# A two-layer hybrid decoder step: sums of weight pieces, normalized x and quarter sums move from GpSimd to VectorE, and the first group of eight hidden tiles is computed without Strassen

## The chip, the cores and the metric

The kernel runs on one core of a Trainium2 chip. The engines are TensorE (PE: matmuls; PEld is its weight load), VectorE (DVE), ScalarE (ACT), GpSimd (POOL) and SyncE (SP, which issues the weight loads). Each works off a queue of its own in order and waits on semaphores. The metric is device time in microseconds (us) of one execution; less is better.

## The reference, cut to what matters

Two groups of tokens, 512 of a prompt and 8 x 8 of samples, go through two layers. A layer is a mixer (untouched here) and then a gated MLP with a convolution over three tokens on the gate:

```
h = rmsnorm(x, norm_ffn[l])
gate, fbuf = causal_dwconv(h @ w_ffn_gate[l], ffn_conv_w[l], st_fconv[l])
x = x + (jax.nn.silu(gate) * (h @ w_ffn_up[l])) @ w_ffn_down[l]
```

with `rmsnorm(x, g) = x * rsqrt(mean(x * x) + EPS) * g`, D_MODEL = 1024 and D_FF = 2816. All is float32.

## The kernel before

**Layout.** Features lie on the 128 partitions, the 576 tokens in the free dimension; x is 8 tiles of 128 features (`KT`), the hidden layer 22 tiles (`FT`). Tokens are halved into two products of 288 columns (`HALVES`). A float32 product is made of three matmuls in fp32r: each operand is split into a high part (`whi`, `xh`, `fh`, `nh`, `hh`), a rounding copy on ScalarE, and a low part (`wlo`, `xl`, `fl`, `nl`, `hl`), a subtraction on VectorE, and hi x hi, hi x lo and lo x hi are added up in PSUM (`mm3`).

**Weights.** `plan` lists all weight pieces in the order in which TensorE uses them. A piece is one output tile by half of its input features, [128, 4, 128], and feeds 24 matmuls (4 blocks, 2 token halves, 3 parts). `_Weights` loads pieces by SyncE into rings (`wraw`, `wrax`), splits each into whi and wlo (`_split`; 6 buffers of each) and runs ahead of TensorE (`pump`).

**The MLP.** The hidden tiles go in three groups (`FGS`: 8, 8 and 6). For each group there are gate and up products (tile m = 2j is the gate of hidden tile j, m = 2j + 1 its up), then the down products of this group, which add onto x. Gate tail of j: convolution in three steps (`gcv`, the first on ScalarE), tanh on ScalarE, the product that makes silu (`gth`). Up tail of j: product of gate and up from PSUM (`gp`, one for each token half), then the split into `hh` and `hl`, which the down products read. The down products begin with two output tiles on hidden tiles 0 to 3 of the group, then the same two on 4 to 7 (mode `kouter`).

**Raw, then normalized.** The norm needs all of x, so the first `RAW` = 3 hidden tiles of a layer (six output tiles) are computed from x without its factor R (`fh`, `fl`), and R is applied afterwards (`scaled`, and two products in the gate tail). Meanwhile the normalized x is made: a scaled copy on ScalarE into the space of hh and hl, a product with R on GpSimd, then the split into `nh` and `nl` (`normed`).

**Strassen on the gates.** From hidden tile `PLAIN` = 6 on, gates are made two at a time by Strassen's scheme on quarters (`quad`): 7 products of 12 matmuls instead of 8. Its weight operands are sums of pieces (`post` in `plan`, computed by `_Weights._next` on GpSimd, 4 per pair: `wsum` and three times `wraw`), its x operands are sums of quarters of the normalized x (`quarters`: four differences on GpSimd, then a split into the space of `fh` and `fl`). In the reading of the products one addition into `gpad` is on GpSimd too.

**What sets the order.** The code is run once to record the instructions. A planner holds modelled clocks of the engines; streams (generators such as `gate_tail`, `up_tail`, `quarters`) are advanced between matmuls (`tick`), the one with the earliest modelled start first, and streams that share the 5 temporary tiles (`take`, `give`) wait for a free one. The recorded order of each engine is then fixed, and each engine works off its own in order. `drain` advances streams until the named ones are done: of the quarter sums before the first Strassen pair, of all up tails of a group before the down products read hidden tiles 4 to 7.

Of the kernel before, what the change touches and what calls it, by code (L numbers as in the profile page):

```python
# [27 lines left out]
RAW, PLAIN = 3, 6  # L28
# [72 lines left out]
class _Weights:  # L101
# [53 lines left out]
    def _next(self):  # L155
# [9 lines left out]
        for dst, a, b, op in p["post"]:  # L165
# [3 lines left out]
            self.nc.gpsimd.tensor_tensor(out=self.raw[dst], in0=self.raw[a], in1=self.raw[b], op=op)  # L169
# [14 lines left out]
    def pump(self):  # L184

        while self.ns < len(self.pieces) and self.ns <= self.at + self.BUFS - 2 \
                and self.upto[self.ns] - self.upto[max(self.at, 0)] <= 4:
            src = self.pieces[self.ns]["src"]
            if self.there.get(src, 0.0) > self.nc.vector.plan.now:
                break  # L190
            self._next()
# [49 lines left out]
class _Trunk:  # L241
# [1353 lines left out]
    def build(self):  # L1595
# [94 lines left out]
        for l in range(L):  # L1690
# [55 lines left out]
            for gi, g in enumerate(groups):  # L1746
# [9 lines left out]
            early, late = ([self.px.tile([128, 4, NT], dt, name=n + i, tag=n + i) for n in ("hh", "hl")]  # L1756
                           for i, dt in (("0", F32R), ("1", F32)))
            hid = list(map(_Halves, early))
# [5 lines left out]
            def whole(k):  # L1764

                return late[k // 4][:, k % 4]

            def normed(k):
                w = whole(k)
                S.activation(out=w, in_=xr[:, k], func=AF.Copy, scale=self.p(l, "gffn", k, k + 1))  # L1770
                yield
                nc.gpsimd.tensor_tensor(out=w, in0=w, in1=self.R, op=ALU.mult)
                yield
                S.activation(out=nh[:, k], in_=w, func=AF.Copy)
                yield
                V.tensor_tensor(out=nl[:, k], in0=w, in1=nh[:, k].bitcast(F32), op=ALU.subtract)

            def quarters(k):

                u, w = whole(k), whole(k + 4)  # L1780
                (b11, b12), (b21, b22) = (u[:, 0:HC], u[:, HC:NT]), (w[:, 0:HC], w[:, HC:NT])
                P = nc.gpsimd
                P.tensor_tensor(out=b11, in0=b12, in1=b11, op=ALU.subtract)
                P.tensor_tensor(out=b12, in0=b22, in1=b12, op=ALU.subtract)
                P.tensor_tensor(out=b22, in0=b22, in1=b11, op=ALU.subtract)
                P.tensor_tensor(out=b21, in0=b21, in1=b22, op=ALU.subtract)
                yield
                for i, y in enumerate((u, w)):
                    y = y.rearrange("p (h i) -> p h i", h=2)
# [3 lines left out]
                    V.tensor_tensor(out=tl, in0=y, in1=th.bitcast(F32), op=ALU.subtract)  # L1793

# [335 lines left out]
```

## Time and profile before

| | |
|---|---|
| median of 3 runs | 1524.88 us (1524.59 to 1526.04) |
| profiled execution | 1523.45 us, of it 1521.7 us from the first to the last instruction (the span) |
| PE busy in the span | 1478.8 us (97%), 11428 matmuls |
| DVE busy | 1063.8 us (70%) |
| ACT busy | 680.3 us (45%) |
| POOL busy | 346.5 us (23%) |
| TensorE's mean granted clock | 0.988 of 2.4 GHz |

Matmuls overlap in TensorE, so one of 288 columns has about 0.29 us in the profile while the next starts 0.13 us later; dense work is read from starts, or from the chain of work, not from the busy share. The rows further down are of the first layer; the second layer's MLP lies 747.5 us later.

### The profile page before, as it was taken

Reading aid. Unit: us, or ns where it says so; the run is one execution under the profiler, and the core shown is the slowest. Engines: PE = TensorE matmul, PEld = TensorE weight load, DVE = VectorE, ACT = ScalarE, POOL = GpSimd, SP = SyncE. Lnnn points to the kernel's source line nnn. Section 1 sums busy time; section 2 is a strip of 40 time slices with the busy share of each in tenths; the row PEclk is TensorE's granted clock in tenths of the full one; section 3 lists DMA queues with packets and bytes.
Section 4 is the critical chain, followed back from the end, with each engine's and each line's share of the span. In section 5 each row is a group of like instructions: output and inputs, shape, how many; then the busy total and the mean of one; then the engine's idle time right before and its main releaser. Section 6 shows DMA issues by size and latency. Waiting matters only on the chain.

```text
span 1521.7 us, 29630 instructions
## 1 busy us (share of the span) xinstructions
PE 1478.8 (97%) x11428; PEld 1433.2 (94%) x11428; DVE 1063.8 (70%) x2256; ACT 680.3 (45%) x1449; POOL 346.5 (23%) x749
## 2 busy tenths in 40 slices
PE   8999999999899999999999999999989999999997
PEld 7998898899899999999999988989989999999997
DVE  6887776666973687377667887766588647854866
ACT  5445565545441344134524546754445324432442
POOL 2111023305520231122012111232083013301410
PEclk9999999999999999999999999999999999999998
DMA  5211122332223223222422112025212322232222
GB/s 187 65 56 50 47 74 78 114 119 71 84 77 101 67 98 91 84 85 80 139 80 70 57 42 89 25 85 171 77 56 90 94 74 98 77 92 97 77 80 86
DMA packets 67278, 128.78 MB, mean 85 GB/s; under 512 B 7952, under 2 KB 13248, under 8 KB 67136
## 3 DMA queue, kind: packets, MB, share of 16 engines
q1 hardware_dynamic: 59808, 105.15, 21.9%
q0 software_dynamic: 6208, 20.56, 3.7%
q8 instruction: 89, 1.46, 0.4%
q10 hardware_dynamic: 1120, 1.18, 0.2%
q14 instruction: 53, 0.43, 0.1%
HBM read 116.36 MB, written 10.49 MB: 83 GB/s over the span
## 4 chain that ended last, share of the span: by engine, by line
PE 89%; DVE 7%; issue 1%; ACT 1%; DMA 1%; POOL 1%; DVEq 0%; ACTq 0%; POOLq 0%
PE ps L458 75%; PE q L458 12%; PE ps L229 2%; DVE wlo L229 1%; DVE gcv L229 1%; DMA wraw<-in_w_in_dram 1%; DVE m L229 1%; DVE nl L229 1%; DVE cv L229 1%; ACT m L229 1%; DVE sqacc L229 1%; DVE xr L229 0%; POOL kr_t L229 0%; DVE gth L229 0%; POOL qr_t L229 0%
## 5 line engine op out<-in xcount | busy, mean ns | idle before, releaser
L229 DVE TENSOR_TENSOR wlo<-wraw,whi 128x512 fp32r<-128x512 f32 (+1 forms) x432 | 316.9, 748 | 79.4 <-ACT whi L229 78.1
L229 ACT ACTIVATE whi<-wraw 128x512 fp32r<-128x512 f32 (+1 forms) x432 | 257.6, 613 | 159.8 <-PE ps L458 147.4
L458 PE MATMUL ps<-xh,whi 128*128 128x288 f32 x768 | 244.7, 319 | 4.4 <-ACT xh L229 3.7
L458 PE MATMUL ps<-xl,whi 128*128 128x288 f32 x768 | 229.7, 299 | 0.3 <-DVE xl L229 0.3
L458 PE MATMUL ps<-xh,wlo 128*128 128x288 f32 x768 | 228.7, 298 | 0.4 <-DVE wlo L229 0.4
L458 PE MATMUL ps<-nh,wlo 128*128 128x288 f32 x704 | 209.4, 297 | 13.3 <-DVE wlo L229 13.3
L458 PE MATMUL ps<-nh,whi 128*128 128x288 f32 x704 | 210.0, 298 | 0.0
L458 PE MATMUL ps<-nl,whi 128*128 128x288 f32 x704 | 209.4, 298 | 0.0
L458 PE MATMUL ps<-hh,whi 128*128 128x288 f32 x704 | 208.5, 296 | 0.0
L458 PE MATMUL ps<-hl,whi 128*128 128x288 f32 x704 | 207.6, 295 | 0.0
L458 PE MATMUL ps<-hh,wlo 128*128 128x288 f32 x704 | 207.0, 294 | 0.0
L458 PEld LDWEIGHTS ps<-xh,whi 128*128 128x128 f32 x768 | 146.6, 191 | 15.2 <-issue 7.7
L458 PEld LDWEIGHTS ps<-xl,whi 128*128 128x128 f32 x768 | 147.2, 192 | 0.8 <-DVE xl L229 0.7
L458 PEld LDWEIGHTS ps<-xh,wlo 128*128 128x128 f32 x768 | 147.0, 191 | 0.9 <-DVE wlo L229 0.9
L458 PEld LDWEIGHTS ps<-nh,wlo 128*128 128x128 f32 x704 | 134.5, 191 | 13.8 <-DVE wlo L229 13.8
L229 DVE SCALAR_TENSOR_TENSOR xr<-ps,xr 128x288 f32<-128x288 f32 x96 | 41.4, 457 | 139.4 <-PE ps L458 139.1
L458 PEld LDWEIGHTS ps<-nl,whi 128*128 128x128 f32 x704 | 133.8, 190 | 0.0
L458 PEld LDWEIGHTS ps<-nh,whi 128*128 128x128 f32 x704 | 133.8, 190 | 0.0
L458 PEld LDWEIGHTS ps<-hh,wlo 128*128 128x128 f32 x704 | 132.5, 188 | 0.0
L458 PEld LDWEIGHTS ps<-hl,whi 128*128 128x128 f32 x704 | 132.1, 188 | 0.0
L458 PEld LDWEIGHTS ps<-hh,whi 128*128 128x128 f32 x704 | 131.9, 187 | 0.0
L229 POOL TENSOR_TENSOR wraw<-wraw,wraw 128x512 f32<-128x512 f32 x48 | 76.9, 1602 | 106.9 <-DVE wlo L229 82.3
(310 smaller groups left out, 3327.0 us busy)
## 6 DMA issues: line engine op xcount, KB each, us to landing
wraw<-in_w_gu_dram SPq DMA_DIRECT2D x176, 256.0 KB, 2.9
wraw<-in_w_in_dram SPq DMA_DIRECT2D x96, 256.0 KB, 2.7
wraw<-in_w_dn_dram SPq DMA_DIRECT2D x80, 256.0 KB, 2.8
wraw<-in_w_out_dram SPq DMA_DIRECT2D x32, 256.0 KB, 2.9
xr<-in_x_dram POOLq DMA_DIRECT2D x12, 288.0 KB, 6.2
vs<-in_st_delta_dram POOLq DMA_DIRECT2D x6, 512.0 KB, 4.1
out_s_delta_dram<-vs POOLq DMA_DIRECT2D x6, 512.0 KB, 3.1
spill<-xr POOLq DMA_DIRECT2D x8, 288.0 KB, 2.5
```

Of the source, the lines that this page charges most:

```text
L229: return f(*args, **kw)
L458: self.nc.raw.tensor.matmul(out, lhsT, rhs, start=start, stop=stop)
```

## The change

It does four things.

- `RAW` goes from 3 to 5 and `PLAIN` from 6 to 8: ten output tiles of group 0 come from raw x, six plain ones from normalized x, and group 0 has no Strassen pair. Seven pairs a layer remain, in groups 1 and 2.
- The normalized x is one VectorE instruction for each of 8 tiles (x times weight times R, into a temporary tile `nx`), then split as before; hh and hl are no longer lent to it.
- The quarter sums are made on VectorE: x is put together again from nh and nl (`qu`, `qw`), and four differences follow, two of them after the first split. They are queued after the last gate and up product of group 0 and drained before the first Strassen pair of group 1.
- The sums of weight pieces and the addition in the reading of the Strassen products go to VectorE. `pump` now asks for all loads that a piece's sums need, not for its own alone.

```
-RAW, PLAIN = 3, 6
+RAW, PLAIN = 5, 8
...
-            self.nc.gpsimd.tensor_tensor(out=self.raw[dst], in0=self.raw[a], in1=self.raw[b], op=op)
+            self.nc.vector.tensor_tensor(out=self.raw[dst], in0=self.raw[a], in1=self.raw[b], op=op)
...
-            src = self.pieces[self.ns]["src"]
-            if self.there.get(src, 0.0) > self.nc.vector.plan.now:
+            p = self.pieces[self.ns]
+            if max(self.there.get(k, 0.0) for k in (p["src"], *p["need"])) > self.nc.vector.plan.now:
...
             def normed(k):
-                w = whole(k)
-                S.activation(out=w, in_=xr[:, k], func=AF.Copy, scale=self.p(l, "gffn", k, k + 1))
+
+                yield self.take(1)
+                w = self.temp("nx")
+                V.scalar_tensor_tensor(out=w[:, 0:NT], in0=xr[:, k], scalar=self.p(l, "gffn", k, k + 1), in1=self.R,
+                                       op0=ALU.mult, op1=ALU.mult)
                 yield
-                nc.gpsimd.tensor_tensor(out=w, in0=w, in1=self.R, op=ALU.mult)
+                S.activation(out=nh[:, k], in_=w[:, 0:NT], func=AF.Copy)
                 yield
...
-                P = nc.gpsimd
-                P.tensor_tensor(out=b11, in0=b12, in1=b11, op=ALU.subtract)
-                P.tensor_tensor(out=b12, in0=b22, in1=b12, op=ALU.subtract)
-                P.tensor_tensor(out=b22, in0=b22, in1=b11, op=ALU.subtract)
-                P.tensor_tensor(out=b21, in0=b21, in1=b22, op=ALU.subtract)
-                yield
+                yield self.take(2)
+                u, w = self.temp("qu"), self.temp("qw")
+                for t, i in ((u, k), (w, k + 4)):
+                    V.tensor_tensor(out=t[:, 0:NT], in0=nh[:, i].bitcast(F32), in1=nl[:, i].bitcast(F32), op=ALU.add)
+                (b11, b12), (b21, b22) = ((t[:, 0:HC], t[:, HC:NT]) for t in (u, w))
                 for i, y in enumerate((u, w)):
-                    y = y.rearrange("p (h i) -> p h i", h=2)
+                    if i == 0:
+                        V.tensor_tensor(out=b11, in0=b12, in1=b11, op=ALU.subtract)
+                        V.tensor_tensor(out=b12, in0=b22, in1=b12, op=ALU.subtract)
+                    else:
+                        V.tensor_tensor(out=b22, in0=b22, in1=b11, op=ALU.subtract)
+                        V.tensor_tensor(out=b21, in0=b21, in1=b22, op=ALU.subtract)
+                    yield
...
-                    nc.gpsimd.tensor_tensor(out=t, in0=t, in1=v, op=ALU.add)
+                    V.tensor_tensor(out=t, in0=t, in1=v, op=ALU.add)
...
                         self.drain(*s_nx)
-                        s_q = [self.add(quarters(k)) for k in range(4)]
-                    elif g == 0 and gr["mode"] == "quad" and s_q:
+                    elif gr["mode"] == "quad" and s_q:
                         self.drain(*s_q)
                         s_q = None
...
                 if g == last_g:
                     self.squares()
+                elif g == 0:
+                    s_q = [self.add(quarters(k)) for k in range(4)]
```

**Place 1: VectorE at the first piece on normalized x, first layer.** Names: `wlo` is a piece's low half, `gcv` and `gth` belong to a gate tail, `gp` is a product of gate and up, `gpad` a gate copied from PSUM. Before, the low half of the first normalized piece is `wlo76`:

```order
L229 SCALAR_TENSOR_TENSOR gcv_4936<-gpad_4917,prm0_91,gcv_4936 128x592 x2
L229 SCALAR_TENSOR_TENSOR gcv_4925<-gth_4940,gcv_4925 128x592
L229 TENSOR_TENSOR gth_4940<-gcv_4925,rn_87 128x512
L229 TENSOR_TENSOR gth_4940<-gcv_4925,rn_87 128x64
L229 TENSOR_TENSOR gp_4945<-ps_4558,gth_4927 128x288
L229 TENSOR_TENSOR gp_4945<-ps_4648,gth_4927 128x288
L229 TENSOR_TENSOR wlo76_4949<-wraw76_4781,whi76_4948 128x512
L229 TENSOR_TENSOR wlo77_4981<-wraw77_4813,whi77_4980 128x512
```


After, the first normalized piece is 84, since pieces 76 to 83 are on raw x:

```order
L229 TENSOR_TENSOR wlo83_5204<-wraw83_5056,whi83_5203 128x512
L229 TENSOR_TENSOR hl0_4522<-gp_5197,hh0_4520 128x576
L229 TENSOR_TENSOR gpad_5235<-ps_5169,rn_87 128x288
L229 TENSOR_TENSOR gpad_5235<-ps_5175,rn_87 128x224
L229 TENSOR_TENSOR gpad_5235<-ps_5175,rn_87 128x8x8
L229 TENSOR_TENSOR wlo84_5242<-wraw84_5096,whi84_5241 128x512
L229 SCALAR_TENSOR_TENSOR gcv_5263<-gpad_5235,prm0_91,gcv_5263 128x592 x2
L229 TENSOR_TENSOR wlo85_5280<-wraw85_5135,whi85_5279 128x512
```


Two gate tails and a product stood in front of the first normalized low half; now the copy of one gate does.

**Place 2: VectorE at the end of group 0's gate and up products, first layer.** `gp` and `hl1` of the eighth hidden tile are what the down products wait for. Before:

```order
L229 SCALAR_TENSOR_TENSOR gth_5754<-gth_5754,gcv_5700 128x512
L229 SCALAR_TENSOR_TENSOR gth_5754<-gth_5754,gcv_5700 128x64
L229 TENSOR_TENSOR gp_5788<-ps_5647,gth_5754 128x288
L229 TENSOR_TENSOR gp_5788<-ps_5651,gth_5754 128x288
L229 TENSOR_TENSOR wlo101_5795<-wraw98_5645,whi101_5794 128x512
L229 TENSOR_TENSOR gp_5804<-ps_5727,gth_5738 128x288
L229 TENSOR_TENSOR gp_5804<-ps_5731,gth_5738 128x288
L229 TENSOR_TENSOR hl1_5436<-gp_5788,hh1_5435 128x576
L229 TENSOR_TENSOR hl1_5436<-gp_5804,hh1_5435 128x576
L229 TENSOR_TENSOR wlo102_5834<-wraw99_5687,whi102_5833 128x512
```


After, the gate tail of the eighth tile (`gcv_5699`, `gth_5733`) and the first rows of the quarter sums (`qu`, `qw`):

```order
L229 SCALAR_TENSOR_TENSOR gcv_5699<-gpad_5671,prm0_91,gcv_5699 128x592 x2
L229 TENSOR_TENSOR wlo97_5716<-wraw97_5574,whi97_5715 128x512
L229 SCALAR_TENSOR_TENSOR gth_5733<-gth_5733,gcv_5699 128x512
L229 SCALAR_TENSOR_TENSOR gth_5733<-gth_5733,gcv_5699 128x64
L229 TENSOR_TENSOR wlo98_5750<-wraw98_5608,whi98_5749 128x512
L229 TENSOR_TENSOR qu_5759<-nh_4524,nl_4525 128x576
L229 TENSOR_TENSOR qw_5760<-nh_4524,nl_4525 128x576
L229 TENSOR_TENSOR qu_5759<-qu_5759 128x288
L229 TENSOR_TENSOR qu_5759<-qw_5760,qu_5759 128x288
```


After, the last rows of the quarter sums and what follows them (`gp_5859` is the product of the eighth tile):

```order
L229 TENSOR_TENSOR qw_5836<-qw_5836 128x288
L229 TENSOR_TENSOR fl_4050<-qu_5843,fh_4049 128x576
L229 TENSOR_TENSOR qw_5844<-qw_5844,qu_5843 128x288
L229 TENSOR_TENSOR qw_5844<-qw_5844 128x288
L229 TENSOR_TENSOR fl_4050<-qw_5836,fh_4049 128x576
L229 TENSOR_TENSOR gp_5859<-ps_5683,gth_5733 128x288
L229 TENSOR_TENSOR gp_5859<-ps_5687,gth_5733 128x288
L229 TENSOR_TENSOR fl_4050<-qw_5844,fh_4049 128x576
L229 TENSOR_TENSOR hl1_4523<-gp_5859,hh1_4521 128x576
```


The product of the eighth tile stood right behind the gate tails and a piece's low half; now 31 instructions of quarter sums and one piece's low half stand between its gate tail and it.

**Place 3: TensorE at the third piece of the first down products, first layer, with the semaphores waited for.** `hh1` and `hl1` hold hidden tiles 4 to 7. Before:

```order
L458 MATMUL ps_5807<-hl1_5436,whi101_5794 128x288
L458 MATMUL ps_5807<-hh1_5435,wlo101_5795 128x288
L458 MATMUL ps_5800<-hh1_5435,whi101_5794 128x288 [waits Activation_49]
L458 MATMUL ps_5800<-hl1_5436,whi101_5794 128x288 [waits DVE_49]
L458 MATMUL ps_5800<-hh1_5435,wlo101_5795 128x288
```


After:

```order
L458 MATMUL ps_5771<-hl1_4523,whi98_5749 128x288
L458 MATMUL ps_5771<-hh1_4521,wlo98_5750 128x288
L458 MATMUL ps_5755<-hh1_4521,whi98_5749 128x288 [waits Activation_49]
L458 MATMUL ps_5755<-hl1_4523,whi98_5749 128x288 [waits DVE_49]
L458 MATMUL ps_5755<-hh1_4521,wlo98_5750 128x288
```


Nothing moved on TensorE here: in both, the two waits in the middle are those for the eighth hidden tile's high part (ScalarE) and low part (VectorE).

## Rows read from the trace of the kernel before

**Rows 1.** TensorE's waits, longest first: waiter <- releaser: us in total, times, longest.

```profile
PE ps L458 <- DVE wlo L229: 13.7, 4, 6.7
```

**Rows 2.** The chain that ended last, in order of time: start us, us, what.

```profile
389.17 40.45 PE ps L458 x286
429.61 11.12 PE q L458 x84
440.74 64.00 PE ps L458 x480
```

**Rows 3.** TensorE in order of time: start us, us, instruction, idle before and its releaser.

```profile
382.09 0.30 PE L458 MATMUL ps<-nh,whi 128*128 128x288 f32 x1
...
389.17 0.61 PE L458 MATMUL ps<-nh,wlo 128*128 128x288 f32 x1 [6.65 <-DVE wlo L229]
...
453.37 0.30 PE L458 MATMUL ps<-hh,whi 128*128 128x288 f32 x1
```

**Rows 4.** VectorE in order of time, end of the raw stretch.

```profile
355.61 0.68 DVE L229 TENSOR_TENSOR wlo<-wraw,whi 128x512 fp32r<-128x512 f32 x1
...
376.78 0.87 DVE L229 TENSOR_TENSOR gpad<-ps,rn 128x288 f32<-128x288 f32 x3
377.58 1.69 DVE L229 SCALAR_TENSOR_TENSOR gcv<-gpad,prm,gcv 128x592 f32<-128x592 f32 x2
...
382.46 2.10 DVE L229 SCALAR_TENSOR_TENSOR gcv<-gpad,prm,gcv 128x592 f32<-128x592 f32 x2
...
388.43 1.89 DVE L229 TENSOR_TENSOR wlo<-wraw,whi 128x512 fp32r<-128x512 f32 x2
```

**Rows 5.** GpSimd in order of time, a Strassen stage.

```profile
519.49 1.71 POOL L229 TENSOR_TENSOR wraw<-wraw,wraw 128x512 f32<-128x512 f32 x1
```

**Rows 6.** VectorE in order of time, the same Strassen stage.

```profile
519.97 1.79 DVE L229 TENSOR_TENSOR wlo<-wraw,whi 128x512 fp32r<-128x512 f32 x1
521.68 1.69 DVE L229 SCALAR_TENSOR_TENSOR gcv<-gpad,prm,gcv 128x592 f32<-128x592 f32 x2
523.29 0.82 DVE L229 SCALAR_TENSOR_TENSOR gth<-gth,gcv 128x512 f32<-128x512 f32 x2
524.03 0.68 DVE L229 TENSOR_TENSOR wlo<-wraw,whi 128x512 fp32r<-128x512 f32 x1
...
531.12 0.81 DVE L229 TENSOR_TENSOR gp<-ps,gth 128x288 f32<-128x288 f32 x2
531.85 0.68 DVE L229 TENSOR_TENSOR wlo<-wraw,whi 128x512 fp32r<-128x512 f32 x1
533.20 0.69 DVE L229 TENSOR_TENSOR wlo<-wraw,whi 128x512 fp32r<-128x512 f32 x1 [0.68 <-ACT whi L229]
533.81 0.45 DVE L229 TENSOR_TENSOR gpad<-qw,q 128x288 f32<-128x288 f32 x1
534.17 0.75 DVE L229 TENSOR_TENSOR hl<-gp,hh 128x576 fp32r<-128x576 f32 x1
534.84 0.68 DVE L229 TENSOR_TENSOR wlo<-wraw,whi 128x512 fp32r<-128x512 f32 x1
```

**Rows 7.** Stretches behind the idle time: start:end, us, busy (x) by engine, PEclk, DMA.

```profile
389.20:400.00 10.80, 10.80 (x66) 10.80 (x67) 10.73 (x13) 4.32 (x9) 8.62 (x10) 0.79 0.25 73
400.00:411.00 11.00, 11.00 (x85) 11.00 (x84) 8.45 (x13) 6.92 (x16) 1.54 (x5) 1.00 0.52 168
```

**Rows 8.** ScalarE in order of time, a gate tile from PSUM on.

```profile
410.05 0.88 ACT L229 ACTIVATE gpad<-ps 128x288 f32<-128x288 f32 x3 [4.08 <-PE ps L458]
410.81 0.64 ACT L229 ACTIVATE whi<-wraw 128x512 fp32r<-128x512 f32 x1
...
411.91 0.79 ACT L229 ACTIVATE gcv<-gpad,prm 128x592 f32<-128x592 f32 x1
```

**Rows 9.** VectorE in order of time, start of the first down projection.

```profile
453.17 0.86 DVE L229 TENSOR_TENSOR gp<-ps,gth 128x288 f32<-128x288 f32 x2 [2.42 <-PE ps L458]
453.94 1.60 DVE L229 TENSOR_TENSOR hl<-gp,hh 128x576 fp32r<-128x576 f32 x2
```

More of the change, by code (lines that the diff above doesn't have):

```diff
@@ L1755, in build @@
             nc.gpsimd.dma_start(out=stf, in_=a["st_ffn"][l])
-            early, late = ([self.px.tile([128, 4, NT], dt, name=n + i, tag=n + i) for n in ("hh", "hl")]
-                           for i, dt in (("0", F32R), ("1", F32)))
-            hid = list(map(_Halves, early))
+            hid = [_Halves(*(self.px.tile([128, 4, NT], F32R, name=n + i, tag=n + i) for i in "01")) for n in ("hh", "hl")]
             nh, nl = self.bigtile("nh"), self.bigtile("nl")
@@ L1762, in build @@
             nf = NP_TOK + SB * 10
-            def whole(k):
-                return late[k // 4][:, k % 4]
             def normed(k):
-                w = whole(k)
-                S.activation(out=w, in_=xr[:, k], func=AF.Copy, scale=self.p(l, "gffn", k, k + 1))
+                yield self.take(1)
+                w = self.temp("nx")
+                V.scalar_tensor_tensor(out=w[:, 0:NT], in0=xr[:, k], scalar=self.p(l, "gffn", k, k + 1), in1=self.R,
+                                       op0=ALU.mult, op1=ALU.mult)
@@ L1771, in normed @@
                 yield
-                nc.gpsimd.tensor_tensor(out=w, in0=w, in1=self.R, op=ALU.mult)
+                S.activation(out=nh[:, k], in_=w[:, 0:NT], func=AF.Copy)
                 yield
-                S.activation(out=nh[:, k], in_=w, func=AF.Copy)
-                yield
-                V.tensor_tensor(out=nl[:, k], in0=w, in1=nh[:, k].bitcast(F32), op=ALU.subtract)
+                V.tensor_tensor(out=nl[:, k], in0=w[:, 0:NT], in1=nh[:, k].bitcast(F32), op=ALU.subtract)
+                self.give(w)
@@ L1778, in quarters @@
             def quarters(k):
-                u, w = whole(k), whole(k + 4)
-                (b11, b12), (b21, b22) = (u[:, 0:HC], u[:, HC:NT]), (w[:, 0:HC], w[:, HC:NT])
-                P = nc.gpsimd
-                P.tensor_tensor(out=b11, in0=b12, in1=b11, op=ALU.subtract)
-                P.tensor_tensor(out=b12, in0=b22, in1=b12, op=ALU.subtract)
-                P.tensor_tensor(out=b22, in0=b22, in1=b11, op=ALU.subtract)
-                P.tensor_tensor(out=b21, in0=b21, in1=b22, op=ALU.subtract)
@@ L1787, in quarters @@
-                yield
-                for i, y in enumerate((u, w)):
-                    y = y.rearrange("p (h i) -> p h i", h=2)
+                yield self.take(2)
[3 more added lines that the diff above has]
+                (b11, b12), (b21, b22) = ((t[:, 0:HC], t[:, HC:NT]) for t in (u, w))
+                for i, y in enumerate((u, w)):
+                    if i == 0:
[5 more added lines that the diff above has]
+                    yield
+                    y = y[:, 0:NT].rearrange("p (h i) -> p h i", h=2)
@@ L1793, in quarters @@
                     V.tensor_tensor(out=tl, in0=y, in1=th.bitcast(F32), op=ALU.subtract)
+                self.give(u, w)
             def evac_gu(m, h, ps):
@@ L1850, in hide @@
                 jj = j - [f[0] for f in FGS if f[0] <= j][-1]
-                if jj == 4 and len(hid[0].parts) == 1:
-                    for n, t in zip(("hh", "hl"), hid):
-                        t.parts += (self.px.tile([128, 4, NT], F32R, name=n + "1", tag=n + "1"),)
                 hi, lo = (t[:, jj, :] for t in hid)
```

## The prediction

> **What bounds the kernel now.** I read the list of waits of TensorE first. Its longest entry by far is the wait for VectorE's low halves of the weights, 13.7 us in total, 6.7 us at the longest [rows 1]. The chain of work in order of time says what surrounds it: long dense stretches of matmuls, 64.00 us for 480 of them, so 0.1333 us each [rows 2]. One weight piece is 24 matmuls or 3.2 us, a Strassen pair (84 matmuls) 11.12 us [rows 2], and two plain tiles instead 96 matmuls or 12.8 us. VectorE is an in-order queue beside this: it is free on average and still sets the end wherever something that TensorE needs stands behind something else. So the question is not how much VectorE does, but what stands in front of what.
>
> The one large hole lies where group 0 turns from raw x to normalized x. TensorE starts its first normalized matmul at 382.09, and the third one, the first that reads a low half, only at 389.17, after 6.65 us of idling [rows 3]. VectorE shows why: from 382.46 to 388.4 it works off the gate tails of three tiles and two products, and the low half that TensorE needs is behind them [rows 4]. While it does so, GpSimd runs the quarter sums, and the same VectorE steps take long: a convolution pair of 592 columns 2.10 us here, 1.69 us when GpSimd is quiet [rows 4, 6]. After the hole the granted clock is lower: 0.79 on the mean from 389.2 to 400, then 1.00 again [rows 7]. The 286 matmuls after it took 40.45 us where 0.1333 each gives 38.1: another 2.3 us [rows 2]. All in all the hole is 6.8 us and the clock cost 2.2 to 2.3, once a layer: 13.7 us of waiting in total is twice 6.7 [rows 1].
>
> **What the change does there.** Group 0 stays on raw x for ten output tiles instead of six (RAW 5), then runs six plain tiles on normalized x, with no Strassen pair. Up to 382.09 TensorE's order is the same, and 20 pieces follow, 480 matmuls, 64.0 us: the first down projection could begin at 382.09 + 64.0 = 446.1. Before it began at 453.37 [rows 3]. The 7.3 us are the hole 6.8, plus the clock cost 2.2, less the 12 matmuls more (1.7).
>
> Does the hole come back elsewhere in this stretch? I walked VectorE's new order with the step times of rows 6 (from start to next start): low half 0.61, 576-column sum 0.67, 288-column step 0.36, convolution pair 1.61, gate pair 0.74, product pair with PSUM 0.73. The normalized x on VectorE has no row in the trace; eight steps between 0.67 (a plain 576-column sum) and 0.80 (a 592-column scalar product, half of 1.61); I take 0.76, nearer to the second since it has a scalar pointer too. They start near 356.2, behind the low half at 355.61 [rows 4]. The tightest place is the low half of the third piece after 382.09. Up to and with it VectorE has 8 steps that normalize (6.1), their 8 low halves (5.4), 8 low halves of weights (4.9), three convolutions (4.8), three gates of raw tiles (0.80 + 0.74 each, 4.6), two pairs of products (1.5), two scaled copies of a gate at 0.80 [rows 4] (1.6), one low half of a hidden tile (0.7): 29.6 us, and about 1.4 us of exposed waits on ScalarE's tanh. So it is ready near 387.2 and needed at 382.09 + 2 x 3.2 = 388.5, with 1.3 us to spare. The normalized x itself is complete near 378 and first needed at 382.09 + 8 x 3.2 = 407.7. So the old hole is gone, worth 7.3 us a layer.
>
> The sums of weight pieces in the seven Strassen pairs a layer that remain: four sums of 128x512 and one of 288 columns move to VectorE, 4 x 0.61 + 0.36 = 2.8 us per 23.9 us (11.12 + 12.8). Against that VectorE's own steps no longer stretch: a low half beside GpSimd's sum took 1.79 us, 0.68 to 0.69 elsewhere [rows 5, 6]. TensorE waits for nothing in that stage before, and by the same walk each low half stays 6 us or more ahead. I put it at nothing; if the cover failed, it would show 14 times at up to 2.8 us.
>
> **The new wait.** The quarter sums are now queued when the last matmul of group 0 has been issued. In VectorE's order they stand behind the gate tail of the eighth hidden tile and ahead of that tile's product with its up projection, which the down projection reads as its last quarter (the order fences show it, with TensorE's two waits). VectorE cannot start them early, since the gate tail ahead of them waits for TensorE:
> - the gate matmuls of the eighth tile end at 382.09 + 18 x 3.2 = 439.7;
> - ScalarE copies them out, splits a weight, scales: 0.76 + 0.52 + 0.79 with gaps gives 441.9 [rows 8];
> - VectorE: convolution 1.61, a low half 0.61, the tanh of ScalarE (0.2 of it exposed), gate pair 0.74, a low half 0.61: 445.9;
> - then the block: 8 sums of 576 columns at 0.67, 16 differences of 288 at 0.36 to 0.46 (half of them need the one just before; I take 0.41), 7 low halves of quarters at 0.67, one weight's low half 0.61: 5.4 + 6.5 + 4.7 + 0.6 = 17.2 us, to 463.1;
> - only now the product (0.81), ScalarE's high half (about 0.7 with its gap) and the low half (0.75) [rows 6, 9]: 465.5.
>
> TensorE, meanwhile, starts the down projection at 446.1, runs two pieces on the first four hidden tiles and 18 matmuls of the third piece, and reaches the eighth hidden tile at 446.1 + 66 x 0.1333 = 454.9. It waits 10.6 us. Before, the same step had no quarter sums ahead: the product ran at 453.17, right after the matmuls, its low half was done by 455.5 [rows 9], and TensorE needed it near 462.
>
> Bounds of the block: with every difference at 0.36 and no exposed step it is 16.4 us, with 0.1 us more on each of 31 steps about 20. If GpSimd stretched the steps as in the old hole, it would be over 25; but only small copies are left there. The Trainium skill (SBUF — State Buffer, section Who interferes with whom) says that a VectorE instruction with two SBUF inputs contends with a GpSimd instruction that reads SBUF, and that the later one blocks for its whole length; by that rule the stretched rows belong to the removed GpSimd sums, and the block goes at the short price. The stretched rows above, 1.79 beside 0.69, agree with it.
>
> Clock after the new hole: nothing at the least, twice 2.2 at the most, since the hole is longer; I take the 2.2 that the old one cost.
>
> **The sum, per layer.** -7.3 + 10.6 + 2.2 = +5.5 us. Both layers have the same order in the changed program, so +11.0. The profiled execution took 1523.45 (span 1521.7 and 1.75 around it), so 1534.4; the median of the runs shown is 1.4 higher, 1524.88, and gives **1535.9 us**.
>
> **Rivals.**
> 1. The block is hidden, and only the old hole goes: 1524.88 - 14.6 = 1510.3, faster. For it: nothing in the quarter sums needs the matmuls in front of them, VectorE idles for some microseconds per tile in this stretch, and VectorE loses the contention. Against: the queue is in order. It decides at 435.3: the block would have to start there to end 2.4 us before 454.9, and the gate tail ahead of it cannot be done before 445.9. 0.10. The Trainium skill (GPSIMD Engine Reference, section 4.1 Engine selection) sends two-input elementwise work to VectorE, as about 2 times slower on GpSimd; taken alone it is this rival. The trace agrees on the price of a 128x512 step (1.71 us there [rows 5], 0.69 here [rows 6]), which says nothing on the place.
> 2. Old and new hole cancel: the block at its short price and no clock cost, or a few steps earlier than I have them: within 3 us of before, say 1526. 0.07.
> 3. Slower still: the raw stretch is late. Ten tiles scaled by the norm after the product cost VectorE more than plain copies, and 1.3 us of slack is not much. If its steps from 355 to 387 run as stretched as in the old hole, TensorE waits at that third piece, 2 to 4 us and some clock, on top of the new hole: 1540 to 1547. 0.10.
> 4. VectorE falls behind in the Strassen stage, 1 us at each of 14 pairs, with the new hole: near 1550. 0.03.
>
> **The numbers.** The forecast has 0.70; its own range is 1529 (short block, no clock cost) to 1544 (long block, double clock cost). The 80% range takes in most of rivals 2 and 3: 1525 to 1546. A measurement of this kernel can tell about 0.2%, 3 us, from no change. Slower by more: 0.70 + 0.10 + 0.03 = 0.83. Within: 0.07. Faster: 0.10.
>
> **What will show it.** In the profile after: no gap of TensorE near 382 and 1135; a gap of 9 to 12 us a layer near 455 and 1208, that ends on the eighth hidden tile's high or low half; in front of it VectorE busy without a break on tiles qu, qw and fl; a granted clock below 1 behind it. TensorE has 24 matmuls more. No waits in the Strassen stages. Wrong would be: no gap in the down projection (then rival 1), the product of the last tile ahead of the block, or the old hole at another piece.

## The result, and the profile after

The changed kernel took 1537.32 us (median, 1534.95 to 1537.39), the kernel before 1524.74 us (1524.56 to 1526.04) beside it: ratio 1.0076, 95% interval 1.0064 to 1.0089. It is slower, by 12.6 us, where 11.0 was forecast.

TensorE's waits, longest first (us in total, times, longest). The entry of [rows 1] for VectorE's low halves has gone from the top of the list, and one for the high part of a hidden tile, from ScalarE, stands there:

```profile
PE ps L458 <- ACT hh L229: 18.9, 2, 9.5
```

The chain that ended last (start, us, what), which answers to [rows 2]. One dense piece now spans the raw and the normalized tiles up to the gate of the eighth: 672 matmuls in 89.60 us, 0.1333 each. There the chain leaves TensorE for the eighth gate's tail and the quarter sums, and comes back at 467.20; TensorE's own work goes on to 456.78 meanwhile. The next 317 matmuls take 44.67 us, where 0.1333 each gives 42.3: 2.4 us lost.

```profile
351.75 89.60 PE ps L458 x672
467.20 44.67 PE ps L458 x317
511.87 11.12 PE q L458 x84
...
594.76 64.00 PE ps L458 x480
```

TensorE in order of time (start, us, instruction, idle before and its releaser), which answers to [rows 3]: the first normalized matmul, the first on a hidden tile, and the place of the new hole. It starts a matmul at 456.65, the next, on the eighth tile's high part, at 466.41, and the one on its low part at 467.20. From 456.65 + 0.13 to 467.20, less the one matmul between, that is 10.3 us.

```profile
409.58 0.30 PE L458 MATMUL ps<-nh,whi 128*128 128x288 f32 x1
...
447.98 0.30 PE L458 MATMUL ps<-hh,whi 128*128 128x288 f32 x1
...
456.65 0.29 PE L458 MATMUL ps<-hh,wlo 128*128 128x288 f32 x1
466.41 0.61 PE L458 MATMUL ps<-hh,whi 128*128 128x288 f32 x1 [9.47 <-ACT hh L229]
467.20 0.61 PE L458 MATMUL ps<-hl,whi 128*128 128x288 f32 x1 [0.18 <-DVE hl L229]
```

VectorE in order of time, which answers to [rows 4, 9]: the normalized x, the tight low half of the raw stretch, and the block. The sums run without a break from 447.30 to the eighth tile's product at 464.82, 17.5 us.

```profile
358.10 3.73 DVE L229 SCALAR_TENSOR_TENSOR nx<-xr,prm,rn 128x576 f32<-128x576 f32 x5
...
387.87 1.28 DVE L229 TENSOR_TENSOR wlo<-wraw,whi 128x512 fp32r<-128x512 f32 x2
...
446.70 0.69 DVE L229 TENSOR_TENSOR wlo<-wraw,whi 128x512 fp32r<-128x512 f32 x1
447.30 0.75 DVE L229 TENSOR_TENSOR qu<-nh,nl 128x576 f32<-128x576 f32 x1
...
464.15 0.75 DVE L229 TENSOR_TENSOR fl<-qw,fh 128x576 fp32r<-128x576 f32 x1
464.82 0.82 DVE L229 TENSOR_TENSOR gp<-ps,gth 128x288 f32<-128x288 f32 x2
465.56 0.75 DVE L229 TENSOR_TENSOR fl<-qw,fh 128x576 fp32r<-128x576 f32 x1
466.39 0.76 DVE L229 TENSOR_TENSOR hl<-gp,hh 128x576 fp32r<-128x576 f32 x1
```

Stretches (start:end, us, busy by engine, PEclk, DMA), which answer to [rows 7]. Where the old hole and its lower clock were, TensorE is busy throughout at full clock. In the new hole and behind it the granted clock is 0.81 and 0.78 on the mean, so part of it at 1.2 GHz, after TensorE had idled; then 1.00.

```profile
382.00:389.20 7.20, 7.20 (x57) 7.20 (x56) 7.10 (x14) 3.00 (x6) 0.00 (x0) 1.00 0.12 36
389.20:400.00 10.80, 10.80 (x84) 10.80 (x83) 9.98 (x19) 4.96 (x8) 2.07 (x4) 1.00 0.39 123
...
454.90:466.00 11.10, 2.04 (x16) 1.81 (x14) 10.93 (x22) 3.75 (x6) 0.00 (x0) 0.81 0.00 0
466.00:480.00 14.00, 13.41 (x81) 13.09 (x82) 6.24 (x13) 4.56 (x9) 0.00 (x0) 0.78 0.31 95
480.00:497.00 17.00, 17.00 (x130) 17.00 (x129) 5.68 (x11) 3.57 (x6) 0.00 (x0) 1.00 0.40 125
```

**One number for the stretch.** From here on I use the time between the start of a layer's first raw matmul and the start of the first Strassen product of group 1, read from TensorE's starts. It leaves the mixer out. Before: 342.68 to 504.57, 161.89 us. After: 344.58 to 511.71, 167.13 us, so +5.2 us. The second layer gives the same two numbers within 0.03. Behind the stretch nothing moved: from its end to the second layer's first matmul it is 257.65 us in every profile of this document. So the 13.9 us between the two profiled spans (1535.6 and 1521.7) are 5.2 twice, and 1.9 and 1.6 in the two mixers.

### The profile page after: what moved, and what is told of

Read it like the earlier page. It is cut to its first block, busy times and chain, and to the rows that moved or that the text cites. A ratio compares the mean times of both kernels' runs of the same rounds, so it can differ in the third digit from the quotient of the medians.

```text
span 1535.6 us, 29594 instructions
## 1 busy us (share of the span) xinstructions
PE 1484.8 (97%) x11452; PEld 1437.1 (94%) x11452; DVE 1073.3 (70%) x2384; ACT 669.0 (44%) x1423; POOL 179.6 (12%) x621
## 4 chain that ended last, share of the span: by engine, by line
PE 87%; DVE 7%; ACT 2%; POOL 2%; issue 1%; DMA 1%; DVEq 0%; ACTq 0%; POOLq 0%
PE ps L458 75%; PE q L458 10%; PE ps L229 2%; DMA wraw<-in_w_in_dram 1%; DVE m L229 1%; DVE qw L229 1%; DVE wlo L229 1%; DVE qu L229 1%; ACT m L229 1%; DVE fl L229 1%; DVE cv L229 1%; DVE sqacc L229 0%; DVE xr L229 0%; POOL kr_t L229 0%; ACT vs L229 0%
## 5 line engine op out<-in xcount | busy, mean ns | idle before, releaser
L229 DVE TENSOR_TENSOR wlo<-wraw,whi 128x512 fp32r<-128x512 f32 (+1 forms) x428 | 284.7, 675 | 86.8 <-ACT whi L229 85.1
L458 PE MATMUL ps<-nh,whi 128*128 128x288 f32 x640 | 189.3, 296 | 0.0
L458 PE MATMUL ps<-nl,whi 128*128 128x288 f32 x640 | 188.8, 295 | 0.0
L458 PE MATMUL ps<-nh,wlo 128*128 128x288 f32 x640 | 188.2, 294 | 0.0
L458 PEld LDWEIGHTS ps<-nh,wlo 128*128 128x128 f32 x640 | 120.5, 188 | 0.0
L458 PEld LDWEIGHTS ps<-nl,whi 128*128 128x128 f32 x640 | 120.1, 188 | 0.0
L458 PEld LDWEIGHTS ps<-nh,whi 128*128 128x128 f32 x640 | 119.9, 187 | 0.0
L229 POOL COPY fs<-gpad 128x2 f32<-128x2 f32 x88 | 30.6, 363 | 701.4 <-DVE gpad L229 628.7
```

Source lines behind the costliest of these rows:

```text
L229: return f(*args, **kw)
L458: self.nc.raw.tensor.matmul(out, lhsT, rhs, start=start, stop=stop)
```

## The experiments

The theory: the sums of this prediction, an old hole gone (7.3 us a layer) and a new one made by the place of the quarter sums in VectorE's queue (10.3 us and 2.4 of clock). The rivals: the moved work itself costs, on VectorE or as plain products; or something outside of the hole does. The code cuts leave out the lines that only carry the list `s_q` along. The table has the medians, the ratio to the kernel before as measured beside each, and the stretch defined above (first layer).

| kernel | us | ratio (95%) | stretch | TensorE's gaps in it |
|---|---|---|---|---|
| before | 1524.7 | | 161.89 | 6.8 |
| after | 1537.3 | 1.0076 (1.0064 to 1.0089) | 167.13 | 10.3 |
| e1_sums_late | 1511.7 | 0.991 (0.9893 to 0.9926) | 154.60 | none |
| e7_two_late | 1514.0 | 0.9929 (0.9915 to 0.9944) | 156.20 | 1.5 |
| e2_sums_early | 1514.6 | 0.9936 (0.9921 to 0.9951) | 156.54 | 1.8 |
| e3_posts_pool | 1536.4 | 1.0073 (1.0058 to 1.0088) | 167.06 | 10.3 |
| e5_late_raw3 | 1511.0 | 0.9905 (0.989 to 0.9919) | 154.61 | none |
| e9_raw3_norm_pool | 1517.1 | 0.9952 (0.9936 to 0.9968) | 160.29 | 2.75 |
| e10_raw3_sums_pool | 1536.6 | 1.0075 (1.0058 to 1.0092) | 167.34 | 10.9 |
| e6_late_posts_pool | 1510.0 | 0.9899 (0.9883 to 0.9916) | 154.60 | none |

### The sums behind the eighth tile's product

```
 def hidden(pi, g):
...
                 elif pi == 1:
                     self.release(True)
                     self.flush()
                     self.drain(*ups.values())
+                    if g == 0:
+                        s_q.extend(self.add(quarters(k)) for k in range(4))
...
-                elif g == 0:
-                    s_q = [self.add(quarters(k)) for k in range(4)]
```

> The changed kernel with one thing moved: the quarter sums are queued after the up tails of group 0 are drained, between the second and the third piece of the first down projection, so VectorE has the product and the low half of the eighth hidden tile (gp, hl) ahead of them. Theory (the new hole is the block of quarter sums in front of the eighth tile's product, and the old hole is gone): no gap of TensorE near 456.7 and 1211, hl of the eighth tile ready near 450 and needed near 457, no new wait since 40 us of down products and 25 us of up products follow before the first Strassen pair; time 1537.3 - 2 x (10.3 gap + 2.4 clock) = 1511.9 us, and some 3.4 us less, 1508.5, if what the profiled run of the changed kernel lost outside of the hole was that run's alone. Rival A (the moved work itself costs, by sums and normalized x on VectorE or by plain products in place of Strassen): the gap goes, but the time stays above 1520. Rival B (the block is only moved on, and the weights' low halves behind it come late in the down projection): gap gone at the eighth tile, a new one of 2 to 8 us within the next 20 us, 1517 to 1530.

1511.74 us, 0.2 from what the theory gave. VectorE in order of time: the product and the low half come first, hl is done near 451.8 and is needed near 458.5, and the sums follow beside the down products.

```profile
449.43 0.86 DVE L229 TENSOR_TENSOR gp<-ps,gth 128x288 f32<-128x288 f32 x2 [0.39 <-PE ps L458]
451.05 0.76 DVE L229 TENSOR_TENSOR hl<-gp,hh 128x576 fp32r<-128x576 f32 x1 [0.76 <-ACT hh L229]
...
452.93 0.75 DVE L229 TENSOR_TENSOR qu<-nh,nl 128x576 f32<-128x576 f32 x1
```

No gap is left in the stretch, and it is 161.89 - 154.60 = 7.3 us shorter than before: what the prediction had for the old hole. The same instructions in another place are 25.6 us faster than the changed kernel, and 2 x (10.3 + 2.4) is 25.4. Rivals A and B fall: beyond the 12 more matmuls a layer of the plain products, which the 7.3 us have in them, the moved work costs nothing that can be seen, and no low half comes late behind the sums.

### Half of the sums behind it

```
+                    if g == 0:
+                        s_q.extend(self.add(quarters(k)) for k in (2, 3))
...
-                    s_q = [self.add(quarters(k)) for k in range(4)]
+                    s_q.extend(self.add(quarters(k)) for k in (0, 1))
```

> The changed kernel with half of the quarter sums moved: two of the four streams of quarter sums stay ahead of the eighth hidden tile's product, the other two are queued behind it. Theory (the hole is as long as the block exceeds TensorE's lead): block 8.6 us in place of 17.5, so the product starts near 456 and the low half is done near 458.2, needed near 456.9: gap of 0.6 to 1.5 us in place of 10.3, little or no lower clock behind it; time 1537.3 - 2 x (9.2 + 2.4) = 1514 us, between 1512 and 1517. Rival (the hole is set by something else than the block's length, such as a wait of the first quarter sum or of the tile's gate): gap of 5 us or more, 1525 or above.

1514.01 us. VectorE in order of time, the first sum and the product; then TensorE at the eighth tile:

```profile
445.50 0.75 DVE L229 TENSOR_TENSOR qu<-nh,nl 128x576 f32<-128x576 f32 x1
...
454.23 0.82 DVE L229 TENSOR_TENSOR gp<-ps,gth 128x288 f32<-128x288 f32 x2
```

```profile
454.84 0.29 PE L458 MATMUL ps<-hh,wlo 128*128 128x288 f32 x1
455.82 0.40 PE L458 MATMUL ps<-hh,whi 128*128 128x288 f32 x1 [0.68 <-ACT hh L229]
456.61 0.40 PE L458 MATMUL ps<-hl,whi 128*128 128x288 f32 x1 [0.39 <-DVE hl L229]
```

The block is 8.7 us in place of 17.5, 8.8 less; the gap is 1.5 in place of 10.3, 8.8 less. So the hole is the block's length less a lead of TensorE that is 7.2 us in both, one for one. Behind this short gap the granted clock stays 1.00 (455 to 470 us), and the stretch is just 1.6 us over that of e1_sums_late.

### The sums where the kernel before had them

```
                         self.drain(*s_nx)
+                        s_q = [self.add(quarters(k)) for k in range(4)]
...
-                elif g == 0:
-                    s_q = [self.add(quarters(k)) for k in range(4)]
```

> The changed kernel with the quarter sums at the place where the kernel before has them: queued when the normalized x is complete and the raw tiles are through, beside the first plain tiles on normalized x. In VectorE's order all of the block then stands within the gate and up products of hidden tiles 5 to 7, with the low halves of only four pieces inside and that of the seventh normalized piece behind. Theory (only the place in VectorE's queue counts): the block of 17.5 us and four low halves runs from about 394.5 to 413, the seventh normalized piece is needed near 403.2: a gap of 8 to 10 us per layer there in place of the one at the down projection, time within 4 us of 1537. Rival (beside the products VectorE's idle time hides the block, and the down projection was just a bad place): no gap over 1 us, 1509 to 1514.

1514.59 us: not what I had worked out for the theory, and not quite the rival's either. The miss is in my expectation's arithmetic: I counted the pieces from 384, where normalized x began with RAW 3. With RAW 5 it begins 8 pieces, 25.6 us, later. VectorE and TensorE in order of time:

```profile
407.89 0.75 DVE L229 TENSOR_TENSOR qu<-nh,nl 128x576 f32<-128x576 f32 x1
...
427.79 0.82 DVE L229 TENSOR_TENSOR gp<-ps,gth 128x288 f32<-128x288 f32 x2
428.52 1.89 DVE L229 TENSOR_TENSOR wlo<-wraw,whi 128x512 fp32r<-128x512 f32 x3
```

```profile
427.29 0.29 PE L458 MATMUL ps<-nl,whi 128*128 128x288 f32 x1
429.26 0.40 PE L458 MATMUL ps<-nh,wlo 128*128 128x288 f32 x1 [1.68 <-DVE wlo L229]
```

The block runs from 407.9 to 427.8, the seventh normalized piece stands behind it as expected, and it was needed near 427.4 (408.0 + 6 x 3.2 + 0.27): a gap of 1.8 us. With its start put right, the rule of the queue gives this gap too, though only after the result: 17.5 us of sums and four low halves of 0.61 from 407.9 on, then the product and the low half, end near 429.2. Recorded in one piece like this, the block is 1.8 us too long even there; behind the eighth tile it costs nothing.

### The weight sums back on GpSimd, with the hole and without

The first of the two kernels is the changed one with this edit, the second e1_sums_late with it:

```
-self.nc.vector.tensor_tensor(out=self.raw[dst], ...)
+self.nc.gpsimd.tensor_tensor(out=self.raw[dst], ...)
...
-V.tensor_tensor(out=t, in0=t, in1=v, op=ALU.add)
+nc.gpsimd.tensor_tensor(out=t, in0=t, in1=v, op=ALU.add)
```

> The changed kernel with the sums of weight pieces and the addition in the reading of the Strassen products back on GpSimd; all else as changed. Theory (these sums are hidden on either engine): gap at the eighth hidden tile as in the changed kernel, 10 us per layer, no other; time 1537.3 within 1.5 us; VectorE's low halves take longer again on the mean in the Strassen stages. Rival (the sums on VectorE are what costs the part of the difference that the hole doesn't explain, about 3.4 us): 1533.5 to 1534.5. Rival on the other side (GpSimd beside VectorE stretches VectorE's steps until TensorE waits): gaps in the Strassen stages, over 1540.

> As e1_sums_late (quarter sums behind the eighth tile's product), with the sums of weight pieces and the addition in the reading of the Strassen products back on GpSimd. In a kernel with no hole nothing is left that could cover their price. Theory (28 sums a layer, 2.8 us per Strassen pair, are hidden on either engine): no gap of over 0.5 us in the Strassen stages, 1511.7 within 2 us, VectorE's low halves about 10% longer on the mean. Rival A (on VectorE they cost something): faster than e1_sums_late by 2 us or more. Rival B (GpSimd's sums stretch VectorE's steps until TensorE waits): slower by 2 us or more.

1536.43 and 1510.03 us, each within 2 us of its partner (after, e1_sums_late), with stretches equal to 0.07 us. The sums lie behind that stretch, in the Strassen pairs, and there TensorE shows no gap: to the second layer's first matmul it is 257.65 us in these two, in their partners and in the kernel before. VectorE's low halves as a group (busy us, mean ns), in the changed kernel and then in e3_posts_pool:

```profile
L229 DVE TENSOR_TENSOR wlo<-wraw,whi 128x512 fp32r<-128x512 f32 (+1 forms) x428 | 284.7, 675 | 86.8 <-ACT whi L229 85.1 <-issue 0.2
```

```profile
L229 DVE TENSOR_TENSOR wlo<-wraw,whi 128x512 fp32r<-128x512 f32 (+1 forms) x428 | 302.2, 719 | 93.4 <-ACT whi L229 92.2
```

With the sums on GpSimd a low half is 7% longer on the mean, and TensorE never sees it. This part of the change is worth nothing either way here. The profiled execution of e6_late_posts_pool had its first raw matmul at 342.62, that of e1_sums_late at 346.23: the 3.4 us between these two executions are 3.6 in the first mixer and -0.2 in the second, and not in the sums.

### What closed the old hole

Three kernels have the quarter sums off VectorE's critical place and RAW at 3, where the old hole was. All keep PLAIN at 8: with no Strassen pair in group 0 its sums can wait, and that part was not tested alone. The first changes RAW alone against e1_sums_late, the second makes the normalized x on GpSimd as before, the third the quarter sums.

```
-RAW, PLAIN = 5, 8
+RAW, PLAIN = 3, 8
```

> The changed kernel with the quarter sums behind the eighth tile's product, as in e1_sums_late, and with RAW back at 3: six output tiles on raw x, ten plain ones on normalized x. VectorE's order up to the low half of the third normalized piece is nearly that of e1_sums_late. Theory 1 (the old hole went because VectorE has fewer and shorter steps there: no GpSimd work beside it, normalized x in one pass, other order): the last low half of normalized x comes 35 us after the first raw matmul and is needed at 40, the third normalized piece's low half at 44 and is needed at 46: no gap, 1511.7 within 2 us. Theory 2 (the old hole went because RAW 5 moves the first normalized piece 25.6 us later): a gap of 4 to 7 us per layer at the first normalized pieces, with a lower clock behind it, 1521 to 1530.

1510.98 us and no gap. With PLAIN 8 and the sums late, RAW 5 isn't needed to close the old hole. VectorE's row of the third and fourth normalized low halves: the first is done near 386.9, and needed at 342.92 + 39.41 + 6.4 + 0.27 = 389.0.

```profile
386.23 1.28 DVE L229 TENSOR_TENSOR wlo<-wraw,whi 128x512 fp32r<-128x512 f32 x2
```

```
-V.scalar_tensor_tensor(out=w[:, 0:NT], in0=xr[:, k], scalar=self.p(l, "gffn", k, k + 1), in1=self.R, ...)
+S.activation(out=w[:, 0:NT], in_=xr[:, k], func=AF.Copy, scale=self.p(l, "gffn", k, k + 1))
+yield
+nc.gpsimd.tensor_tensor(out=w[:, 0:NT], in0=w[:, 0:NT], in1=self.R, op=ALU.mult)
```

> As e5_late_raw3 (quarter sums late on VectorE, RAW 3, PLAIN 8), with the normalized x made as before: scaled copy on ScalarE, product with R on GpSimd, then the split. In VectorE's order two gate tails and a product then stand ahead of the first normalized low half again. Theory 1 (place in the queue and GpSimd's steps beside VectorE make the old hole; the quarter sums on GpSimd are gone, so only a part of it comes back): VectorE free of stretched steps from about 35 us after the first raw matmul on, the first normalized low half near 42.5 to 43.5, needed at 39.7: gap of 2.9 to 4.5 us per layer, lower clock worth 0 to 2.2, time 1518 to 1525. Theory 2 (the normalized x on VectorE plays no part, the quarter sums alone made the hole): no gap over 1 us, 1511 to 1514.

1517.11 us, a little under the range, with a gap of 0.5 + 2.25 us where 2.9 to 4.5 was expected. TensorE at the first normalized piece, as in [rows 3]:

```profile
384.26 0.40 PE L458 MATMUL ps<-nh,whi 128*128 128x288 f32 x1 [0.35 <-ACT whi L229]
...
386.86 0.61 PE L458 MATMUL ps<-nh,wlo 128*128 128x288 f32 x1 [2.08 <-DVE wlo L229]
```

So the way in which the normalized x is made is the cause of a part: it put two gate tails ahead of the first normalized low half. Of the 6.8 us of the old hole 2.75 come back. The stretch is 5.7 us over that of e5_late_raw3, so 2.9 went with a lower clock in this execution, which took 1523.52 us; the four executions without a profile took 1516.60 to 1517.77.

The other 4.1 us can be read by comparing rows. The same six rows of VectorE (parts of two gate tails, then the product `gp`) stand ahead of the first normalized low half in the kernel before and here. First the kernel before, where GpSimd runs its quarter sums from 378.54 on and the low half starts at 388.43 [rows 4], then e9_raw3_norm_pool, where GpSimd has only small copies:

```profile
379.18 1.38 DVE L229 SCALAR_TENSOR_TENSOR gcv<-gth,gcv 128x592 f32<-128x592 f32 x1
```

```profile
379.71 0.77 DVE L229 SCALAR_TENSOR_TENSOR gcv<-gth,gcv 128x592 f32<-128x592 f32 x1
...
386.13 1.28 DVE L229 TENSOR_TENSOR wlo<-wraw,whi 128x512 fp32r<-128x512 f32 x2
```

They took 9.25 us beside the sums and 6.42 us without: 2.8 us. VectorE also came to them 1.1 us later, counted from the first raw matmul (36.5 and 35.4 us). That is an estimate from rows of two kernels that differ elsewhere too; no run brings the whole hole back.

The third is e2_sums_early with RAW 3 and `quarters` on GpSimd, so against e5_late_raw3 the sums change both engine and place. There GpSimd also adds nh and nl, 8 steps of 576 columns that the kernel before didn't have.

```
-V.tensor_tensor(out=t[:, 0:NT], in0=nh[:, i].bitcast(F32), in1=nl[:, i].bitcast(F32), op=ALU.add)
+nc.gpsimd.tensor_tensor(out=t[:, 0:NT], in0=nh[:, i].bitcast(F32), in1=nl[:, i].bitcast(F32), op=ALU.add)
...
-V.tensor_tensor(out=b11, in0=b12, in1=b11, op=ALU.subtract)
+nc.gpsimd.tensor_tensor(out=b11, in0=b12, in1=b11, op=ALU.subtract)
...
```

> As e5_late_raw3 but with the quarter sums on GpSimd, queued when the normalized x is complete, as before; GpSimd also puts x together from its two halves. VectorE's order is that of e5_late_raw3, row by row, up to the low half of the fourth normalized piece. So it is a run on whether GpSimd's sums lengthen VectorE's steps beside them, and what that costs. Theory 1 (they do, as in the kernel before): convolution pairs near 2.1 in place of 1.7 us, gate steps 1.4 and 1.9 in place of 0.8 and 0.8, so the third normalized piece's low half comes 4 us later than in e5_late_raw3, where it has 2 us to spare: gap of 2 to 4 us per layer, 1515 to 1522. Theory 2 (the steps in the kernel before were long for another reason): steps as in e5_late_raw3, no gap, time within 2 us of it.

1536.61 us: both numbers missed. VectorE's steps do get longer beside GpSimd's sums. GpSimd starts them at 384.47; the gate steps of 512 and 64 columns took 0.83 us just before and take 1.94 then, a low half 1.92:

```profile
383.49 0.83 DVE L229 TENSOR_TENSOR gth<-gcv,rn 128x512 f32<-128x512 f32 x2
384.24 0.77 DVE L229 SCALAR_TENSOR_TENSOR gcv<-gth,gcv 128x592 f32<-128x592 f32 x1
385.04 1.94 DVE L229 TENSOR_TENSOR gth<-gcv,rn 128x512 f32<-128x512 f32 x2
...
394.03 1.92 DVE L229 TENSOR_TENSOR wlo<-wraw,whi 128x512 fp32r<-128x512 f32 x1
```

They start too late to delay the third piece, where I had expected the gap. The largest gap comes elsewhere, 7.9 us before 424.34, and ends on a high half of ScalarE; the other 3.0 of the 10.9 us end on low halves of VectorE. ScalarE and TensorE in order of time:

```profile
407.60 0.69 ACT L229 ACTIVATE fh<-qu 128x576 fp32r<-128x576 f32 x1 [2.76 <-POOL qu L229]
413.85 0.69 ACT L229 ACTIVATE fh<-qu 128x576 fp32r<-128x576 f32 x1 [5.57 <-POOL qu L229]
416.08 0.69 ACT L229 ACTIVATE fh<-qw 128x576 fp32r<-128x576 f32 x1 [1.54 <-POOL qw L229]
416.67 0.77 ACT L229 ACTIVATE gcv<-gpad,prm 128x592 f32<-128x592 f32 x1
...
423.67 1.13 ACT L229 ACTIVATE whi<-wraw 128x512 fp32r<-128x512 f32 x2
```

```profile
424.34 0.61 PE L458 MATMUL ps<-nh,whi 128*128 128x288 f32 x1 [7.72 <-ACT whi L229]
```

ScalarE splits the sums as GpSimd delivers them (0.8 to 2 us a step), waits 5.6 us for one, and two gate tails, each with a step on VectorE between, stand ahead of the weight's high half. It is the same mechanism in ScalarE's queue: an instruction that waits for a slow producer holds up everything recorded after it. So quarter sums on GpSimd at the early place can cost 10.9 us a layer. This run doesn't part the engine from the place, and the kernel before had fewer sums, so the share of the old hole that was theirs rests on the rows above.

### The part that the hole doesn't explain

> The changed kernel once more, unedited, for the part of the difference that the hole doesn't explain: in its profile the mixers of both layers took 3.5 us more than in the kernel before (1.9 up to the first raw matmul, 1.6 in the second layer), with the same instructions. If that belongs to the change, the first raw matmul starts near 344.6 again and the time is 1537. If it is a matter of the single execution (where the stretches of lower clock fall in the mixer), this run can differ from it by 1 to 4 us there: first raw matmul between 342.7 and 346.3.

> The kernel before once more, unedited, for its mixers. In its first profile the first raw matmul started at 342.68 us, and from the first matmul of the second layer to that layer's first raw matmul 327.95 us went by; in the other profiles so far the one was 342.7 to 346.2 and the other 327.99 or 329.4 to 329.6, with the same instructions. If the mixers' part of the difference belongs to the change, the two numbers are 342.7 and 328.0 again, within 0.3. If it is a matter of the single execution, at least one is off by over 1 us.

The two took 1536.61 and 1524.07 us. Each kernel repeated its own mixers within 0.4 us, nearly as the expectations have it for a part that belongs to the change: after 344.26 to the first raw matmul and 329.45 us in the second layer (344.58 and 329.52 the first time), before 343.01 and 327.95 (342.68 and 327.95). The order of instructions up to the raw stretch is the same in both kernels, but for one MEMSET and one COPY of at most 0.2 us, which GpSimd does at 311.84 in the changed kernel and later in the one before. What differs is where the granted clock falls. The first mixer before, and then after:

```profile
100.00:200.00 100.00, 94.95 (x903) 89.43 (x901) 81.83 (x185) 57.23 (x124) 12.18 (x44) 1.00 0.20 64
200.00:300.00 100.00, 98.59 (x752) 86.99 (x752) 68.06 (x178) 60.10 (x183) 28.64 (x115) 0.98 0.21 71
```

```profile
100.00:200.00 100.00, 94.94 (x889) 89.35 (x888) 81.74 (x186) 57.23 (x124) 12.17 (x44) 0.98 0.19 63
200.00:300.00 100.00, 97.81 (x752) 85.55 (x752) 68.70 (x178) 60.00 (x183) 28.72 (x112) 1.00 0.20 69
```

But kernels with the same mixers spread as widely: to the first raw matmul 342.62 (e6_late_posts_pool) to 346.23 (e1_sums_late), in the second layer 327.99 (e1_sums_late) to 329.59 (e7_two_late, e9_raw3_norm_pool). From 185 to 200 us the granted clock is 0.89 on the mean in four profiles (both of after, e3_posts_pool, e9_raw3_norm_pool), and their first raw matmul starts at 344.26 to 344.58. In the other eight it is 1.00 there, and seven of them start at 342.62 to 343.21; the eighth, e1_sums_late, has 0.88 from 262 to 290 us, where the others have 0.94 or 1.00. So these microseconds go with the place at which the clock drops within the mixer, and the changed mixers can be as short as before: e6_late_posts_pool has 342.62 and 328.17. Why the unedited kernels each kept their place, and what sets it, stays open.

## Why the prediction was right

**The old hole, 7.3 us a layer: right.** The walk along VectorE had the tight low half ready at 387.2; it was ready near 388.5, at a time scale that the mixer had shifted by 1.9, so 386.6. The first down projection began at 447.98 - 1.9 = 446.1, as forecast. Normalized x took 0.73 us a tile, forecast 0.76, and the steps that the walk lists are those of the trace. One reading in it was off: from 382.46 on VectorE had two gate tails and the two halves of one product ahead of the low half, not three tails and two products; no sum uses that count. The credit was too wide in one point: the walk was made for RAW 5, and e5_late_raw3 shows that RAW 3 has no gap either. Of the hole's 6.8 us, 2.75 are shown to belong to the normalized x by way of GpSimd (e9_raw3_norm_pool); 2.8 are put down to the quarter sums there by comparing rows, and no run shows them alone.

**The new hole, 10.6 us forecast, 10.3 measured.** Step by step, with the 1.9 taken off: block from 445.4 (forecast 445.9), 17.5 us long (17.2), low half of the eighth tile done at 465.2 (465.5), TensorE there at 454.9 (454.9). Between the gate tail and the product stand the 31 instructions of the sums and two low halves of weights, as the prediction counts them (the section on the change names one). e1_sums_late and e7_two_late show that the hole is made by this block.

**The clock behind it, 2.2 forecast, 2.4 measured.** Taken from the old hole, and the longer hole cost hardly more. That it came so near is luck in part, since the prediction had no row for a longer hole and its range went from nothing to twice 2.2. It isn't a fixed price: gaps of 1.5 and 1.8 us (e7_two_late, e2_sums_early) had none, and 2.75 us of e9_raw3_norm_pool cost 2.9 in its profile.

**The sum.** -7.3 + 10.3 + 2.4 = +5.4 a layer against 5.5; the stretch says 5.2. The forecast of 1535.9 is 1.4 below the median. The mixers, for which it had no term, took 1.9 and 1.6 us more in the profiled executions. So the two stretches gave 10.4 us where 11.0 was forecast, and part of the closeness of the total is luck: the mixers made up the rest. The prediction's own range, 1529 to 1544, starts from the profiled 1523.45; from the median it would be 1530 to 1546.

**The rivals.** The first, that the block hides, had its price right: 1510.3, and e1_sums_late has 1511.7. It failed at the point that the prediction named, the place in the queue. The second, that the holes cancel, would have needed a shorter block and no lower clock; they were 17.5 and 2.4 us. The Trainium skill (GPSIMD Engine Reference, section 4.1 Engine selection) sends two-input elementwise work to VectorE. The runs agree for the normalized x (e5_late_raw3 and e9_raw3_norm_pool, 1511.0 and 1517.1) and point the same way for the quarter sums at their early place (e2_sums_early and e10_raw3_sums_pool, 1514.6 and 1536.6, though RAW differs too), find no difference for the weight sums (e6_late_posts_pool), and show that the gain hangs on the place: 1511.7 or 1537.3 us with the same instructions. The third and fourth rivals, a late raw stretch and a late Strassen stage, didn't occur; VectorE had 1.9 us to spare at the tightest piece. That GpSimd lengthens VectorE's steps, for which the prediction cited the Trainium skill (SBUF — State Buffer, section Who interferes with whom), is borne out by e10_raw3_sums_pool: 0.83 before and 1.94 us beside the sums.

## What to carry to other kernels

When work moves to a faster engine, ask first what stands behind it in that engine's queue, and when TensorE needs that: a block of work that isn't needed yet costs its length, less the time that TensorE can still work without what stands behind the block. Queue deferred work behind the last product that the next stage reads, not at the first moment at which it may start; here that one place decided between +0.8% and -0.9%. Test each part of a change alone: RAW 5 (with PLAIN 8) and the weight sums, two of the parts here, moved no time.

## What was not expected of the hardware

- The same mixer, in kernels whose order of instructions is the same up to there but for two small steps of GpSimd, took up to 3.6 us more or less to the first raw matmul (342.62 to 346.23), and the granted clock fell below 1 at different places in it.
- A kernel with a gap of 2.75 us a layer took 1523.5 us in the execution with a profile, where the lower clock behind the gap cost 2.9 us a layer, and 1516.6 to 1517.8 in the four others. The mean granted clock was 0.988 in the first and 0.992 to 0.993 in the others, which is the level of e5_late_raw3 (0.992 to 0.995) without a gap; so the drop behind the gap seems to be missing there, though no profile shows the place.
- 28 sums of weight pieces a layer cost the same time on GpSimd and on VectorE, though VectorE's low halves are 7% longer beside GpSimd (719 and 675 ns).
